# The recurrence's added matrix terms: an addition on VectorE before, a second accumulating product on TensorE after

## The chip, the core and the metric

The kernel runs on one core of a Trainium2 chip. A core has TensorE for matrix products (PE in the profile, its weight loads PEld), VectorE (DVE), ScalarE (ACT), GpSimd (POOL) and SyncE (SP), which issues most of the transfers. Products land in PSUM, eight banks of 128 partitions by 512 float32 values; all else is held in SBUF. The metric is the device time of one execution in microseconds (us). Lower is better.

## The reference

The kernel computes a trunk of two layers on 512 tokens of width 1024 in float32: an RWKV-7 time mixer, a SwiGLU feed-forward layer, a gated spatial mixer (SGU) and a second feed-forward layer, each between two RMS norms. The change is in the time mixer. Each of its 16 heads keeps a state S of 64 by 64 and walks the tokens:

```
S_t = S_{t-1} diag(w_t) + (S_{t-1} a_t) b_t^T + v_t k_t^T
y_t = S_t r_t
```

## The kernel before, in words

**Chunked form.** The recurrence isn't walked token by token. The tokens are cut into 8 chunks of 64. For each head and chunk the kernel builds matrices once, by products, masks and a triangular inverse; then it walks the 8 chunks in order, and in each multiplies those matrices by the state and by the chunk's values. Two heads share the 128 partitions (`hd` is 0 or 1), and two such pairs (`q`) form a block `b`; there are four blocks. `hh` names the first or second four chunks, and `cc` the chunk among the four.

**Stages.** A block runs through P (projections), E (`early`: decay and scaled vectors), F (`front`), B (`back`), S (`scan`) and N (`finish`: group norm, gate). `PLAN` lists the stages of all blocks in the order in which they are written: the ones that matter here are F0 B0 F1 V0 V1 V2 V3 B1 S0 F2 S1 F3 N0 B2 N1 B3 S2 N2 S3 N3, where V are the value projections.

**front** (from line 677) loads for each of the four units (hh, q) of a block a tile MV of 128 by 2x4x2x64 and a tile BX of 128 by 4x4x64, multiplies (lm, line 709), masks the result into MV on VectorE (712), copies parts into LA and BX on ScalarE (715, 716, 726, 727), and lets GpSimd mask one quarter of BX (717). Quarters 2 and 3 of BX get an identity by transfer (703) on the rows of their own head and products on the other rows.

**back** (from line 731) inverts: LA is transposed (LX, line 735), a loop of 15 steps on VectorE (744, 746) solves all diagonal blocks of 16 at once, two transposes follow (749, 750), and a chain of small products with copies between (Qp, Np, Tp, Q2p, T2p) assembles the inverse into bdT. The copies that matter below are the two halves of Q2 (792 on ScalarE, 793 on VectorE) and the two of T2p into bdT (802, one on each engine). Then, for each unit: product mp (807), ScalarE's copy into MVt (809), and for each of the two heads four products gh (814) into one PSUM bank; VectorE adds to the gh bank's first half the quarter 2 or 3 of BX and writes MV[0] (816), and to its second half the old MV[1] and writes MV[1] (817).

**scan** (from line 819) walks the chunks. Each chunk has four products us (843; not in the last chunk), one for each pair and head, whose result times the decay is the next state, in part by VectorE (845) and in part by ScalarE (848), and four products Yp (856). After two chunks ScalarE copies Yp out (858). The values of each chunk are loaded into the state tile by SP (828).

**Who waits for whom.** A scheduler sets each engine's order from the program and a timing model of its own; on the chip each engine then keeps that order. Tiles share buffers: MV, BX and others, such as the tiles of the output projection's operand (oT), share 17 slots, and a tile gets a slot when the last use of an earlier tile is over. A block needs eight slots for MV and BX. The gh banks are two, used in turn.

Of the kernel before, what the change touches and what calls it, by code (L numbers as in the profile page):

```python
# [11 lines left out]
ALU = mybir.AluOpType  # L12

P = 128
# [5 lines left out]
C = 64  # L20
# [62 lines left out]
class Trunk:  # L83
# [287 lines left out]
    def rwkv(self, x0, nxt):  # L371
        nc, i, tc = self.nc, self.i, self.tc
        v, a, g = nc.vector, nc.scalar, nc.gpsimd
        mm = nc.tensor.matmul
        with ExitStack() as ctx:
# [20 lines left out]
            def xslot(name, shape, dt=F32):  # L396
                return self.xp.tile(shape, dt, name=name, tag="x", bufs=TT)

            def gslot(name, shape):
                return self.gp.tile(shape, F32, name=name, tag="gain", bufs=2)  # L400
# [93 lines left out]
            head = [slice(0, 64), slice(64, 128)]  # L494
# [3 lines left out]
            for t, m, w in ((w1m[0], omix, v), (w1m[1], self.vec["mix"], g)):  # L498
                mv = m[:, 3 * KT:5 * KT].rearrange("p (j k) -> p k j", j=2).unsqueeze(3)
# [6 lines left out]
            for j, src in enumerate((hk, hs)):  # L506
                for kt in range(KT):
                    mm(acc, w1m[j][:, kt].rearrange("p j n -> p (j n)"), src(kt), start=j == 0 and kt == 0,
                       stop=j == 1 and kt == KT - 1)
# [220 lines left out]
            def back(b, o):  # L730

                MV, BX, LA, Dm = (o[n] for n in ("MV", "BX", "LA", "Dm"))
# [19 lines left out]
                for hh in range(2):  # L752
                    mt = gslot("MVt", [P, 2, 4, P])
                    for q in q2:
                        pt = self.bank("pl", "mvt")
# [8 lines left out]
                for u in range(16):  # L764
                    for z, hd, x in quarters:
                        mm(Qp[z:z + 32, u * 32:(u + 1) * 32], LAu[z:z + 32, u, 32 * x:32 * x + 32], Dn[z:z + 32, u, x, :],
                           start=True, stop=True)
# [19 lines left out]
                for u in range(16):  # L787
                    for z in (0, 64):
                        mm(Q2p[z + 32:z + 64, u * 32:(u + 1) * 32], LAu[z:z + 32, u, 32:64], Dn2[z:z + 32, u, :],
                           start=True, stop=True)  # L790
# [4 lines left out]
                for u in range(16):  # L795
                    for hd in q2:
                        z = 64 * hd
                        mm(T2p[z:z + 32, u * 32:(u + 1) * 32], Q2[z + 32:z + 64, u, :], bdT[z + 32:z + 64, u, hd, 32:64],
                           start=True, stop=True)
# [4 lines left out]
                for hh, q in units:  # L804
                    mp, mt, mv, bx = self.bank("mp" if b else "pt", "mp"), MVt[hh, q], MV[hh, q], BX[hh, q]
                    for cc in range(4):
                        mm(mp[:, cc * P:(cc + 1) * P], bdT[:, q * NC + 4 * hh + cc].rearrange("p h t -> p (h t)"), mt[:, cc, :],  # L807
                           start=True, stop=True)
                    a.copy(mt.rearrange("p c f -> p (c f)"), mp)
                    for hd in range(2):  # L810
                        rows, other = head[hd], head[1 - hd]
                        gh = self.bank("pt", "gh")
                        for cc in range(4):
                            mm(gh[:, cc * P:(cc + 1) * P], mt[rows, cc, :], bx[rows, 0:2, cc, :], start=True, stop=True)  # L814
                        gv = gh.rearrange("p (c a t) -> p a c t", c=4, a=2)
                        v.tensor_tensor(mv[:, 0, :, hd], gv[:, 0], bx[:, 2 + hd], op=ALU.add)
                        v.tensor_tensor(mv[:, 1, :, hd], gv[:, 1], mv[:, 1, :, hd], op=ALU.add)

            def scan(b, o, then=None):

                MV, pc = o["MV"], o["pc"]
                Y = xslot("Y", [P, TT, 2, P])

                def new_su(c):
                    su = rp.tile([P, 2, 2, C], F32, name="su", tag="su", bufs=4)
                    vv = Vd[c * C:(c + 1) * C, 2 * b * P:2 * b * P + 2 * P].rearrange("t (q h v) -> t q h v", q=2, h=2)
                    for hd in range(2):
                        nc.sync.dma_start(out=su[64 * (1 - hd):64 * (1 - hd) + 64, :, hd, :], in_=vv[:, :, hd, :])
                        if c == 0:
                            g.memset(su[64 * hd:64 * hd + 64, :, hd, :], 0.0)  # L830
                    return su

                su = new_su(0)
                for c in range(NC):
                    hh, cc = c // 4, c % 4
                    tt, par = c // 2, c % 2
                    if c < NC - 1:
                        nsu = new_su(c + 1)
                        us = self.bank("us", "us")
                        for q in q2:  # L840
                            for hd in range(2):
                                rows = slice(64 * hd, 64 * hd + 64)
                                mm(us[rows, q * C:(q + 1) * C], MV[hh, q][:, 0, cc, hd, :], su[:, q, hd, :], start=True, stop=True)

                        v.tensor_tensor(nsu[0:64, :, 0, :], us[0:64, 0:2 * C].rearrange("p (q v) -> p q v", q=2),
                                        pc[0:64, :, c:c + 1].broadcast_to([64, 2, C]), op=ALU.mult)
                        for q in q2:
                            a.activation(nsu[64:128, q, 1, :], us[64:128, q * C:(q + 1) * C], AF.Copy,
                                         scale=pc[64:128, q, c:c + 1])
                    if par == 0:  # L850
                        yp = self.bank("yp", "Yp")
                    yr = slice(64 * par, 64 * par + 64)
                    for q in q2:
                        for hd in range(2):
                            yc = slice(q * P + hd * C, q * P + hd * C + C)
                            mm(yp[yr, yc], MV[hh, q][:, 1, cc, hd, :], su[:, q, hd, :], start=True, stop=True)  # L856
                    if par == 1:
                        a.copy(Y[:, tt].rearrange("p q f -> p (q f)"), yp[:, 0:2 * P])
                    if c < NC - 1:
                        su = nsu  # L860
                    if then and c == NC // 2 - 1:
                        then(Y)
                return Y
# [86 lines left out]
            for n in PLAN:  # L950
                f, b = n[0], int(n[1])
                if f == "P":
                    if xr is None:
                        xr = mixed_split(0, "ssssssss")
                        xx.clear()
                    kr[b] = kr_proj(b)
                elif f == "E":
                    ops[b] = early(b, *kr[b])
                elif f == "X":
                    xs = mixed_split(2, XV)  # L960
                elif f == "V":
                    v_proj(xs, [b])
                elif f == "F":
                    front(b, ops[b])
                elif f == "B":
                    back(b, ops[b])
                elif f == "S":
                    Y[b] = scan(b, ops[b], (lambda y: finish_half(b, ops[b], y, (0, 1))) if b == 3 else None)
                elif b == 3:
                    finish_half(b, ops[b], Y[b], (2, 3))  # L970
                else:
                    finish(b, ops[b], Y[b])
# [166 lines left out]
```

## Time and profile before

| | us |
|---|---|
| median of three runs (1421.11 to 1426.13) | 1424.42 |
| the profiled execution, its own time | 1426.41 |
| its span, first to last instruction | 1424.70 |
| from the first product of block 0's `front` to the end of the last scan, about | 195 to 477 |
| VectorE's additions of lines 816 and 817, 32 each, busy | 13.4 and 13.3 |
| the scan's products of lines 843 and 856, busy | 17.0 and 28.2 |

The page of the profile gives for each engine the busy time and its share, for each line the number of instructions and the mean length of one, and for each wait what ended it. A float32 product of this kernel shows as two records on PE and two on PEld: line 843 has 112 products (7 chunks, 4 products, 4 blocks) and 224 records. "PEclk" is the granted clock of TensorE as a share of full speed. A busy time on PE covers the pipeline's fill and drain, so short gaps are not seen in it.

### The profile page before, as it was taken

How to read it: one execution, taken by the hardware profiler on the slowest of the kernel's cores; microseconds unless marked ns; L12 is line 12 of the kernel's file. 1: busy time of each engine (PE TensorE's matmuls, PEld its weight loads, DVE VectorE, ACT ScalarE, POOL GpSimd, SP SyncE). 2: the span in 40 equal slices, each digit the busy share in tenths (PEclk: the TensorE clock that was granted, in tenths of full speed). 3: DMA queues.
4: the chain of work that ended last, by engine and by line, in shares of the span. 5: the costliest groups of instructions: out<-in, count | busy, mean ns of one | idle time of the engine just before them, and what ended most of it. 6: DMA issues, size and time to landing. Idle time of an engine off the chain costs nothing.

```text
span 1424.7 us, 21481 instructions
## 1 busy us (share of the span) xinstructions
PE 1338.3 (94%) x8472; PEld 1091.2 (77%) x8472; DVE 791.8 (56%) x1318; ACT 569.1 (40%) x1060; POOL 274.5 (19%) x248
## 2 busy tenths in 40 slices
PE   5899997987889979999999999999999999999998
PEld 3576686976768768888888888778888888888886
DVE  6962776388685775554544222865575455443223
ACT  5654665363723363323322122743363232322221
POOL 6154463133311231111111000210121111110000
PEclk9999998987969989999999999999999999999999
DMA  5133467351322423333332232343213333332331
GB/s 157 30 107 92 127 182 200 94 150 43 87 65 88 130 90 104 89 89 103 90 99 94 89 118 74 104 129 109 89 52 112 103 89 89 103 90 103 89 96 67
DMA packets 210324, 143.04 MB, mean 100 GB/s; under 512 B 59664, under 2 KB 185136, under 8 KB 210224
## 3 DMA queue, kind: packets, MB, share of 16 engines
q1 hardware_dynamic: 208544, 135.90, 32.2%
q0 software_dynamic: 1680, 5.77, 1.3%
q8 instruction: 67, 1.10, 0.3%
q14 instruction: 33, 0.27, 0.1%
HBM read 125.39 MB, written 14.16 MB: 98 GB/s over the span
## 4 chain that ended last, share of the span: by engine, by line
PE 77%; DVE 7%; ACT 2%; issue 2%; DMA 2%; POOL 1%; SPq 1%; DVEq 0%; POOLq 0%; ACTq 0%
PE gu L158 12%; PE gu L156 12%; PE gu L157 12%; PE acc L156 8%; PE acc L157 8%; PE acc L158 8%; PE gh L814 2%; PE lm L709 2%; PE u L156 1%; PE u L158 1%; PE u L157 1%; PE Yp L856 1%; PE mp L807 1%; PE proj L158 1%; PE proj L156 1%
## 5 line engine op out<-in xcount | busy, mean ns | idle before, releaser
L131 ACT CAST whi<-wraw 128x1024 fp32r<-128x1024 f32 x161 | 168.8, 1050 | 472.5 <-PE gu L157 257.2
L132 DVE TENSOR_TENSOR wlo<-wraw,whi 128x1024 fp32r<-128x1024 f32 x161 | 246.6, 1532 | 197.2 <-ACT whi L131 193.2
L157 PE MATMUL gu<-hT,whi 128*128 128x512 f32 (+1 forms) x768 | 289.6, 378 | 4.4 <-DVE hT L59 4.4
L156 PE MATMUL gu<-hT,whi 128*128 128x512 f32 (+1 forms) x768 | 290.2, 380 | 0.8 <-ACT hT L57 0.8
L158 PE MATMUL gu<-hT,wlo 128*128 128x512 f32 (+1 forms) x768 | 289.7, 378 | 0.0
L157 PEld LDWEIGHTS gu<-hT,whi 128*128 128x128 f32 x768 | 146.0, 190 | 34.0 <-DVE hT L59 4.7
L156 PEld LDWEIGHTS gu<-hT,whi 128*128 128x128 f32 x768 | 145.8, 191 | 29.5 <-ACT hT L57 1.0
L158 PEld LDWEIGHTS gu<-hT,wlo 128*128 128x128 f32 x768 | 145.8, 190 | 29.0 <-issue 0.2
L157 PE MATMUL acc<-wlo,act 128*128 128x512 f32 x416 | 163.9, 394 | 0.0
L156 PE MATMUL acc<-whi,act 128*128 128x512 f32 x416 | 163.6, 394 | 0.0
L158 PE MATMUL acc<-whi,act 128*128 128x512 f32 x416 | 160.5, 394 | 0.0
L333 POOL TENSOR_TENSOR sg<-sg,hn 128x512 f32<-128x512 f32 x44 | 56.7, 1288 | 422.5 <-DVE sg L332 422.5
L332 DVE TENSOR_TENSOR sg<-sg,gu 128x512 f32<-128x512 f32 x44 | 30.2, 687 | 142.5 <-PE gu L158 141.1
L148 POOL TENSOR_TENSOR wlo<-wraw,whi 128x1024 fp32r<-128x1024 f32 x28 | 70.1, 2505 | 169.9 <-ACT whi L147 151.1
L158 PEld LDWEIGHTS acc<-whi,act 128*128 128x128 f32 x416 | 78.2, 188 | 18.1
L156 PEld LDWEIGHTS acc<-whi,act 128*128 128x128 f32 x416 | 78.2, 188 | 18.0
L157 PEld LDWEIGHTS acc<-wlo,act 128*128 128x128 f32 x416 | 78.1, 188 | 18.0
L330 DVE TENSOR_TENSOR sg<-gu,hn 128x512 f32<-128x512 f32 x44 | 30.4, 691 | 67.8 <-PE gu L158 67.6
L131 ACT CAST act<-sg 128x512 fp32r<-128x512 f32 x52 | 32.3, 622 | 72.2 <-POOL sg L333 58.1
L158 PE MATMUL proj<-xsp,wlo 128*128 128x512 f32 x128 | 53.7, 421 | 0.0
L156 PE MATMUL proj<-xsp,whi 128*128 128x512 f32 x128 | 51.9, 405 | 0.4 <-ACT k L529 0.4
L709 PE MATMUL lm<-MV,ST 128*128 128x128 f32 x256 | 41.6, 316 | 11.2 <-DMA ST<-sb 7.9
(305 smaller groups left out, 2248.8 us busy)
## 6 DMA issues: line engine op xcount, KB each, us to landing
wraw<-in_ffn_w_gate_dram SPq DMA_DIRECT2D x44, 512.0 KB, 3.6
wraw<-in_ffn_w_up_dram SPq DMA_DIRECT2D x44, 512.0 KB
wraw<-in_ffn_w_down_dram SPq DMA_DIRECT2D x44, 512.0 KB, 3.6
wraw<-in_rwkv_w_rkv_dram SPq DMA_DIRECT2D x24, 512.0 KB, 3.5
wraw<-in_sgu_w_in_dram SPq DMA_DIRECT2D x16, 512.0 KB, 3.6
x<-in_x_dram SPq DMA_DIRECT2D x8, 512.0 KB, 3.7
MV<-sa SPq DMA_DIRECT2D x64, 64.0 KB, 2.6
ST<-sb SPq DMA_DIRECT2D x8, 512.0 KB, 4.5
```

Of the source, the lines that this page charges most:

```text
L131: self.nc.scalar.copy(hi, src)
L132: self.nc.vector.tensor_tensor(lo, src, hi.bitcast(F32), op=ALU.subtract)
L148: nc.gpsimd.tensor_tensor(lo, raw, hi.bitcast(F32), op=ALU.subtract)
L156: mm(out, lhs[0], rhs[0], start=start, stop=False)
L157: mm(out, lhs[0], rhs[1], start=False, stop=False)
L158: mm(out, lhs[1], rhs[0], start=False, stop=stop)
L330: nc.vector.tensor_tensor(sg, pp[0], yb, op=ALU.mult)
L332: nc.vector.tensor_tensor(sg, sg, pp[1], op=ALU.mult)
L333: nc.gpsimd.tensor_tensor(sg, sg, yb, op=ALU.mult)
L709: mm(lm[:, cc * P:(cc + 1) * P], st[:, cc].rearrange("p n t -> p (n t)"), mv[:, :, cc, hd, :], start=True, stop=True)
L807: mm(mp[:, cc * P:(cc + 1) * P], bdT[:, q * NC + 4 * hh + cc].rearrange("p h t -> p (h t)"), mt[:, cc, :], start=True, stop=True)
L814: mm(gh[:, cc * P:(cc + 1) * P], mt[rows, cc, :], bx[rows, 0:2, cc, :], start=True, stop=True)
```

## The change

Nothing else than `back` and `scan` is touched. In `back` the additions of lines 816 and 817 are gone. The gh products of both heads are written first, each into its own bank, and then ScalarE makes four plain copies: the first half of each bank into MV[0], the second half into quarter `hd` of BX, whose old contents the products have read by then. MV[1] keeps what `front` put there. In `scan` each product becomes two that accumulate in PSUM: the state times quarter 2 or 3 of BX and then times MV[0], and the state times MV[1] and then times quarter `hd` of BX. BX is thus still read at the last chunk; before, its last reader was in `back`.

```diff
                     a.copy(mt.rearrange("p c f -> p (c f)"), mp)
+                    ghs = [self.bank("pt", "gh") for _ in range(2)]
                     for hd in range(2):
-                        rows, other = head[hd], head[1 - hd]
-                        gh = self.bank("pt", "gh")
                         for cc in range(4):
-                            mm(gh[:, cc * P:(cc + 1) * P], mt[rows, cc, :], bx[rows, 0:2, cc, :], start=True, stop=True)
-                        gv = gh.rearrange("p (c a t) -> p a c t", c=4, a=2)
-                        v.tensor_tensor(mv[:, 0, :, hd], gv[:, 0], bx[:, 2 + hd], op=ALU.add)
-                        v.tensor_tensor(mv[:, 1, :, hd], gv[:, 1], mv[:, 1, :, hd], op=ALU.add)
+                            mm(ghs[hd][:, cc * P:(cc + 1) * P], mt[head[hd], cc, :], bx[head[hd], 0:2, cc, :], start=True, stop=True)
+                    for hd in range(2):
+                        gv = ghs[hd].rearrange("p (c a t) -> p a c t", c=4, a=2)
+                        a.copy(mv[:, 0, :, hd], gv[:, 0])
+                        a.copy(bx[:, hd], gv[:, 1])
...
-                                mm(us[rows, q * C:(q + 1) * C], MV[hh, q][:, 0, cc, hd, :], su[:, q, hd, :], start=True, stop=True)
+                                out = us[rows, q * C:(q + 1) * C]
+                                mm(out, BX[hh, q][:, 2 + hd, cc, :], su[:, q, hd, :], start=True, stop=False)
+                                mm(out, MV[hh, q][:, 0, cc, hd, :], su[:, q, hd, :], start=False, stop=True)
...
-                            mm(yp[yr, yc], MV[hh, q][:, 1, cc, hd, :], su[:, q, hd, :], start=True, stop=True)
+                            mm(yp[yr, yc], MV[hh, q][:, 1, cc, hd, :], su[:, q, hd, :], start=True, stop=False)
+                            mm(yp[yr, yc], BX[hh, q][:, hd, cc, :], su[:, q, hd, :], start=False, stop=True)
```

The scheduler also orders the engines' work anew. Three places show it.

VectorE in block 1's inverse, from ScalarE's and VectorE's copies of Q2 (line 793) to the last copy into bdT (line 802), which the products mp wait for. Names: tm and Dm belong to the solving loop of the next block, mu, va, nr and Y to block 0's group norm. Before, 18 instructions stand between the two copies; the last nine and the copy are

```order
L712 TENSOR_TENSOR MV<-lm,mk_126 64x4x2x64
L173 SCALAR_TENSOR_TENSOR nr_t<-nr_t,nr_a 128x16
L746 TENSOR_TENSOR Dm<-Dm,tm 128x2x13x3
L174 SCALAR_TENSOR_TENSOR nr_y<-nr_t,nr_y 128x16
L744 TENSOR_TENSOR tm<-LX,Dm 128x2x48
L885 TENSOR_TENSOR Y<-Y,nr_y 128x1024
L746 TENSOR_TENSOR Dm<-Dm,tm 128x2x12x4
L744 TENSOR_TENSOR tm<-LX,Dm 128x2x55
L746 TENSOR_TENSOR Dm<-Dm,tm 128x2x11x5
L802 COPY bdT<-T2p 32x16x32
```

and in the changed kernel all of it is

```order
L793 COPY Q_2948<-Q2p 32x512
L881 TENSOR_REDUCE mu<-Y 128x16
L882 TENSOR_SCALAR mu<-mu 128x16
L883 TENSOR_TENSOR Y<-Y,mu 128x1024
L712 TENSOR_TENSOR MV<-lm,mk_126 64x4x2x64
L887 TENSOR_REDUCE va<-hn 128x16
L802 COPY bdT<-T2p 32x16x32
```

The solving loop of the next block now begins after the copy into bdT, and block 0's group norm begins where it had been half done.

TensorE in the first scan, the state's step from the fourth chunk to the fifth. Before, with `front`'s products lm of block 2 behind it:

```order
L843 MATMUL us_3123<-su_3104,MV_1478 64x64 x2
L843 MATMUL us_3123<-su_3104,MV_1485 64x64 x2
L856 MATMUL Yp_3115<-su_3104,MV_1485 64x64
L709 MATMUL lm_3230<-MV_3191,ST_3189 128x128 x4
L709 MATMUL lm_3239<-MV_3191,ST_3189 128x128 x4
```

and in the changed kernel, where the eight rows of the same step are followed by eight Yp rows and then by two rows of lm:

```order
L845 MATMUL us_3147<-su_3120,BX_1514 64x64
L846 MATMUL us_3147<-su_3120,MV_1478 64x64
L845 MATMUL us_3147<-su_3120,BX_1514 64x64
L846 MATMUL us_3147<-su_3120,MV_1478 64x64
L845 MATMUL us_3147<-su_3120,BX_1545 64x64
L846 MATMUL us_3147<-su_3120,MV_1485 64x64
L845 MATMUL us_3147<-su_3120,BX_1545 64x64
L846 MATMUL us_3147<-su_3120,MV_1485 64x64
```

Each product of the step is two rows now; the order of the stages around them is nearly the same.

SP in the second scan, where it loads block 3's MV (line 690) and BX and the state tiles su. Before:

```order
L690 DMA MV_3483<-sa_120 64x4x64 x4
L603 DMA g2_4748<-in_rwkv_g2_dram 128x256
L690 DMA MV_3492<-sa_120 64x4x64 x2
L828 DMA su_3405<-Vd_116 64x2x64 x2
L690 DMA MV_3492<-sa_120 64x4x64 x2
L936 DMA od_125<-ob_3703 128x512
L909 DMA g2r_4754<-in_rwkv_g2_dram 32x256 x3
L828 DMA su_3421<-Vd_116 64x2x64 x2
L690 DMA MV_3499<-sa_120 64x4x64 x2
```

and in the changed kernel, where su_3561 is the second scan's last state tile:

```order
L690 DMA MV_3603<-sa_120 64x4x64
L829 DMA su_3561<-Vd_116 64x2x64 x2
L690 DMA MV_3603<-sa_120 64x4x64 x3
L690 DMA MV_3612<-sa_120 64x4x64 x4
L690 DMA MV_3619<-sa_120 64x4x64 x4
L703 DMA BX_3632<-ident_79 64x4x64 x2
L703 DMA BX_3663<-ident_79 64x4x64 x2
L703 DMA BX_3694<-ident_79 64x4x64 x2
L703 DMA BX_3725<-ident_79 64x4x64 x2
L891 DMA hn_4258<-Vd_116 128x4x256
L829 DMA su_4711<-Vd_116 64x2x64 x2
```

Three of block 3's four MV tiles, spread through the second scan before, now stand behind its last state tile, because BX of blocks 1 and 2 holds its slots longer.

More of the change, by code (lines that the diff above doesn't have):

```diff
@@ L809, in back @@
                     a.copy(mt.rearrange("p c f -> p (c f)"), mp)
+                    ghs = [self.bank("pt", "gh") for _ in range(2)]
                     for hd in range(2):
-                        rows, other = head[hd], head[1 - hd]
-                        gh = self.bank("pt", "gh")
                         for cc in range(4):
-                            mm(gh[:, cc * P:(cc + 1) * P], mt[rows, cc, :], bx[rows, 0:2, cc, :], start=True, stop=True)
-                        gv = gh.rearrange("p (c a t) -> p a c t", c=4, a=2)
-                        v.tensor_tensor(mv[:, 0, :, hd], gv[:, 0], bx[:, 2 + hd], op=ALU.add)
-                        v.tensor_tensor(mv[:, 1, :, hd], gv[:, 1], mv[:, 1, :, hd], op=ALU.add)
+                            mm(ghs[hd][:, cc * P:(cc + 1) * P], mt[head[hd], cc, :], bx[head[hd], 0:2, cc, :], start=True, stop=True)
[3 more added lines that the diff above has]
+                        a.copy(bx[:, hd], gv[:, 1])
             def scan(b, o, then=None):
-                MV, pc = o["MV"], o["pc"]
+                MV, BX, pc = o["MV"], o["BX"], o["pc"]
                 Y = xslot("Y", [P, TT, 2, P])
```

## The prediction

> **What bounds the kernel now.** I read the page's busy line and its chain first, to learn which engine sets the end of the whole program, and then cut the time mixer's scans into stages, because a share over the whole span hides them. The page's busy line, and the chain of waits that ended last:
>
> ```profile
> PE 1338.3 (94%) x8472; PEld 1091.2 (77%) x8472; DVE 791.8 (56%) x1318; ACT 569.1 (40%) x1060; POOL 274.5 (19%) x248
> ...
> PE 77%; DVE 7%; ACT 2%; issue 2%; DMA 2%; POOL 1%; SPq 1%; DVEq 0%; POOLq 0%; ACTq 0%
> ```
>
> TensorE is busy 94% of the span and holds 77% of the chain. So work added to TensorE is likely to cost its full length, and work taken from VectorE pays only in the 7%. The view of six stretches (busy time of each engine, number of records, granted clock) says where either holds:
>
> ```profile
> core 0: us, PE busy (x) PEld busy (x) DVE busy (x) ACT busy (x) POOL busy (x), PEclk, DMA share, GB/s
> 260.00:311.00 51.00, 49.45 (x619) 44.86 (x618) 31.51 (x69) 30.75 (x81) 13.35 (x22) 0.98 0.48 131
> 311.00:345.00 34.00, 21.82 (x411) 19.53 (x401) 26.83 (x55) 13.02 (x32) 12.71 (x13) 0.63 0.21 59
> 345.00:380.00 35.00, 33.98 (x592) 28.68 (x591) 19.45 (x45) 19.88 (x59) 5.45 (x11) 0.97 0.28 67
> 380.00:412.00 32.00, 20.97 (x224) 17.72 (x214) 31.50 (x65) 12.66 (x22) 13.45 (x8) 0.63 0.28 92
> 412.00:441.00 29.00, 27.18 (x536) 22.12 (x536) 13.01 (x26) 11.35 (x26) 0.00 (x0) 0.88 0.19 57
> 441.00:511.00 70.00, 68.46 (x538) 55.59 (x536) 52.46 (x128) 29.41 (x73) 19.77 (x18) 1.00 0.36 111
> ```
>
> There are two regimes. In stretches 1, 3, 5 and 6 TensorE idles 1.55, 1.02, 1.82 and 1.54 us: it is the bound, and VectorE has room. In 2 and 4, where the inverses of blocks 1 and 2 are assembled, TensorE idles 12.2 and 11.0 us at a clock of 0.63, and VectorE is busy 26.83 of 34 and 31.50 of 32 us: there a short VectorE queue is worth something. The scans, and so the new products, lie mostly in the first regime.
>
> **The change, part by part.** The sum goes against the profiled execution's own 1426.41 us, which is 1.99 above the median of the three runs.
>
> *The 240 added products.* 7 x 4 x 4 = 112 for the state and 8 x 4 x 4 = 128 for the output, each as large as those of these groups:
>
> ```profile
> L856 PE MATMUL Yp<-su,MV 128*64 128x64 f32 x256 | 28.2, 232 | 0.0
> L843 PE MATMUL us<-su,MV 128*64 128x64 f32 x224 | 17.0, 235 | 0.0
> ```
>
> The mean of 232 to 235 ns is a record's length with fill and drain, and overlaps its neighbours; the spacing is what an added one costs. A chunk of the last scan, and one of the first, on TensorE's timeline:
>
> ```profile
> 461.39 0.45 PE L843 MATMUL us<-su,MV 128*64 128x64 f32 x8
> 461.67 0.63 PE L856 MATMUL Yp<-su,MV 128*64 128x64 f32 x8
> 462.23 0.50 PE L156 MATMUL acc<-whi,oT 128*128 128x512 f32 x1
> ...
> 296.31 0.22 PE L843 MATMUL us<-su,MV 128*64 128x64 f32 x1
> ...
> 298.79 0.50 PE L856 MATMUL Yp<-su,MV 128*64 128x64 f32 x5
> ...
> 299.19 0.40 PE L843 MATMUL us<-su,MV 128*64 128x64 f32 x7
> ```
>
> From 461.39 to the next work at 462.23, 16 records (8 products) take 0.84 us, 0.105 a product. Inside the seven records that end 0.40 after 299.19, the last is 0.22 long, so the others begin 0.18/6 = 0.03 apart, 0.06 a product while another group's records lie between. I take 0.09, nearer to the whole chunk: 240 x 0.09 = **+21.6** (14.4 to 25.2). Nearly all of it lands on a full TensorE. One part does not: the first scan's last chunks run around the gap before this group,
>
> ```profile
> 315.14 0.34 PE L766 MATMUL Qp<-hn,LA 32*32 32x32 f32 x9 [4.05 <-issue]
> ```
>
> whose products now stand ahead of those chunks: some 12 added products fit in the idle 4.05 us, 12 x 0.09 = **-1.1** (0 to -2).
>
> *The 64 additions leave VectorE, 64 copies come to ScalarE.*
>
> ```profile
> L816 DVE TENSOR_TENSOR MV<-gh,BX 128x256 f32<-128x256 f32 x32 | 13.4, 419 | 9.0 <-PE gh L814 8.8
> L817 DVE TENSOR_TENSOR MV<-gh,MV 128x256 f32<-128x256 f32 x32 | 13.3, 415 | 0.0
> ...
> L858 ACT COPY Y<-Yp 128x256 f32<-128x256 f32 x16 | 6.0, 373 | 8.0 <-PE Yp L856 7.7
> ```
>
> VectorE loses 26.7 us of work. In the first regime this is worth nothing. A ScalarE copy of the same shape from PSUM takes 373 ns, so ScalarE gets 64 x 0.373 = 23.9 us. Its busy times of 13 to 31 us in stretches of 29 to 70 cover them: 0. Without that cover, the next unit's copy of mp waits behind four copies, 1.5 us, and TensorE with it; were that to happen at every third of the 16 units, it would be +8 (I allow +5, since the gh banks of the next unit can be filled meanwhile only if ScalarE has emptied them).
>
> *VectorE's order in the two inverses.* mp waits for VectorE's half of the copy into bdT. In block 1 and block 2:
>
> ```profile
> 312.38 1.20 DVE L877 TENSOR_REDUCE mu<-Y 128x16 f32<-128x1024 f32 x1
> ...
> 316.35 1.23 DVE L879 TENSOR_TENSOR Y<-Y,mu 128x1024 f32<-128x1024 f32 x1
> ...
> 319.06 1.22 DVE L883 TENSOR_REDUCE va<-hn 128x16 f32<-128x1024 f32 x1
> ...
> 328.23 0.70 DVE L793 COPY Q<-Q2p 32x512 f32<-32x512 f32 x1
> ...
> 336.68 0.69 DVE L802 COPY bdT<-T2p 32x512 f32<-32x512 f32 x1
> ...
> 385.17 0.70 DVE L793 COPY Q<-Q2p 32x512 f32<-32x512 f32 x1
> ...
> 396.22 0.69 DVE L802 COPY bdT<-T2p 32x512 f32<-32x512 f32 x1
> ```
>
> ```profile
> 337.42 2.07 PE L807 MATMUL mp<-MVt,bdT 128*128 128x128 f32 x8 [5.25 <-DVE bdT L802]
> ...
> 396.96 2.07 PE L807 MATMUL mp<-MVt,bdT 128*128 128x128 f32 x8 [7.30 <-DVE bdT L802]
> ```
>
> In block 1, 7.75 us lie between the end of the Q copy (328.93) and the start of the bdT copy. The changed order leaves five instructions there: the three group-norm passes of 1.20, 1.23 and 1.22, one mask of 0.68 (row below, line 712) and a small one, 4.5 us. That is **-3** (0 to -6, where T2p's own end is met; a mask that waits for lm makes it 0). In block 2, 10.35 us of solving steps and norm go, and nine instructions stand there now, among them two masks, the next block's LX (1.95 below) and two passes of Y, about 7.3 us: **-3** (0 to -7). The group norm that is pushed behind is late next; its result feeds the output projection, which is filler.
>
> *The gh banks.* Emptied by VectorE, they make TensorE wait now and then, and the products run at two speeds:
>
> ```profile
> 293.75 1.71 PE L814 MATMUL gh<-BX,MVt 64*128 64x128 f32 x16
> ...
> 341.15 3.10 PE L814 MATMUL gh<-BX,MVt 64*128 64x128 f32 x16
> ...
> 357.76 1.79 PE L814 MATMUL gh<-BX,MVt 64*128 64x128 f32 x16 [0.70 <-DVE MV L817]
> ```
>
> 0.70 us in block 1 and the like goes: **-1** (0 to -1.5). In block 2, where VectorE is full, the second bank is empty only after the addition at
>
> ```profile
> 406.33 0.41 DVE L817 TENSOR_TENSOR MV<-gh,MV 128x256 f32<-128x256 f32 x1
> ```
>
> though its products had started at 399.77 (below) and ended 3.09 later: **-2** (0 to -4).
>
> ```profile
> 399.77 3.09 PE L814 MATMUL gh<-BX,MVt 64*128 64x128 f32 x16 [0.73 <-ACT MVt L809]
> ```
>
> *The clock.* The same 16 records take 1.71 us at 293.75 and 3.10 at 341.15, after the 5.25 us gap. With shorter gaps some of it comes back: **-1.5** (0 to -4; all of it is a rival).
>
> *The slots.* BX is now held until the scan. Block b+2's eight slots come free with chunks 4 and 8 of block b's scan, and SP issues the loads of block 3's last units behind the state tiles. One issue of BX's identities, and where the chain of block 3's `front` ends now:
>
> ```profile
> 366.06 3.90 SPq L703 DMA_DIRECT2D BX<-ident  x6
> ...
> 378.43 0.68 DVE L712 TENSOR_TENSOR MV<-lm,mk 64x512 f32<-64x512 f32 x1 [1.78 <-PE lm L709]
> ...
> 380.16 1.95 DVE L735 STREAM_TRANSPOSE LX<-LA 128x1024 f32<-128x1024 f32 x1
> ```
>
> One such issue (3.9 us) behind the state tiles, with TensorE's filler of the output projection late as well because its operand waits for a slot: **+4** (0 to +12). Queued behind a late load on SP are the next state tiles, and the scan waits for these.
>
> *Sum.* 21.6 - 1.1 - 3 - 3 - 1 - 2 - 1.5 + 4 = +14.0. On 1426.4 this is 1440.4, and less 1.99 the median is **1438**, 1.0% slower. All low ends together give 14.4 - 2 - 6 - 7 - 1.5 - 4 - 4 = -10 (1414); all high ends 25.2 + 12 + 5 = +42 (1467).
>
> **The rivals.**
>
> *A: faster, by the clock.* If the gaps before mp get so short that the clock stays up, the busy 21.82 and 20.97 us of stretches 2 and 4 shrink by their missing share of 0.37, 8.1 + 7.8 = 15.9 us in place of my 1.5, and the sum is -0.4; with the gaps themselves at their low ends (-13 in place of -6) it is -7.4, a median near **1417**. For it: 3.10 against 1.71. Against it: the solving loop and the masks still come before mp in block 2, and 4.05 us before Qp is of its own. It decides once no gap in these stretches exceeds some 2 us. The Trainium skill, page "TensorE: Matmul & The Clock Gate", section "HAM oscillation — how this bites in real kernels", says that idle gaps over about 3.4 us throttle the engine to half rate again; the 5.25 and 7.30 us gaps, with 3.10 and 3.09 us products behind them, agree, and by that rule this rival needs both gaps under 3.4.
>
> *B: no change.* Busy TensorE is not full TensorE. Weight loads are busy only 44.86 of 51, 28.68 of 35, 22.12 of 29 and 55.59 of 70 us, so some 34 us have no load, and if half of the added products (10.8 us) slip in there, the sum is +3.2 and the median near **1428**. Against it: the chunk above takes 0.84 us for 8 products with nothing between. The Trainium skill, page "Perfetto Trace Analysis", section "Identifying the Most-Contended Engine", calls the matmul row's busy share a poor sign of utilisation and the weight loads' share the better one; its measure here would be 77%, not 94%.
>
> *C: much slower, by the slots.* Block 3's last three units can be loaded only once the second scan has ended: an issue of 3.9 us, and then three `front` units in a row on TensorE, about 3 us each by the 3.10 us that 16 records take at the low clock, before the solve that now starts at 380.16: +13 where I have +4, and no gain in block 2 (-3 and -2 gone): +29, a median near **1453**. For it: VectorE's bdT copy of block 2 stands behind block 3's LX in the order. Against it: MV was held until the scan already.
>
> *D: the second product of a pair waits for the first's result* in PSUM: 0.235 - 0.09 = 0.145 more for each of 240, +35, near **1473**. Against it, the projections add into the same cells every 394 ns record without a gap:
>
> ```profile
> L157 PE MATMUL acc<-wlo,act 128*128 128x512 f32 x416 | 163.9, 394 | 0.0
> ```
>
> **How the numbers follow.** Chances: the forecast 0.53, A 0.20, B 0.13, C 0.11, D 0.03. The forecast's own range, 1429 to 1448, comes from its larger terms missing one way each. For 8 in 10 I go down to A's value and up past C's: **1416 to 1456**. A difference under 0.3% (4.3 us, 1420.1 to 1428.7) can't be told from none. Faster takes A and a little of the forecast's lower end, 0.21; same takes B and the rest of that end, 0.16; slower 0.63.
>
> **What would show it.** Right: the state's and output's lines with twice the records and a mean still near 0.23 us; stretches like 1, 3 and 5 longer by 5 us each with TensorE as full as before; gaps before mp of 2 to 5 us and a clock still under 0.8 there; ScalarE's new copies near 373 ns and never what mp waits for. Wrong: a clock near 1 in the inverses (A); stretches no longer than before with twice the products (B); block 3's LX more than 8 us behind its old place beside the scan (C); pairs spaced over 0.15 us (D). The size fails above all if a chunk's eight added records cost more than they do in a row, because each half of a pair loads other weights.

## The result, and the profile after

The changed kernel takes 1433.16 us (median of six runs, 1429.08 to 1435.03), the kernel before in the same series 1424.03. The ratio is 1.0057, with a 95% interval of 1.0033 to 1.0081: slower by 8.1 us (4.7 to 11.5), and clear of no change. The forecast was 1438, slower, with 13.6 us in place of the 8 to 9 measured. The profiled execution took 1430.03 us, the second lowest of the six.

The page's busy line and the chain of waits of the changed kernel:

```profile
PE 1351.9 (95%) x8952; PEld 1106.6 (77%) x8952; DVE 772.5 (54%) x1254; ACT 588.3 (41%) x1124; POOL 272.9 (19%) x248
...
PE 71%; DVE 5%; issue 1%; ACT 1%; DMA 0%; POOL 0%; DVEq 0%; POOLq 0%; ACTq 0%
```

The 480 records are there, and so are the 64 additions that VectorE no longer makes and the 64 copies of ScalarE. But TensorE's busy time rose by only 13.6 us. The six stretches of the prediction, in the same columns:

```profile
260.00:311.00 51.00, 50.91 (x691) 46.70 (x684) 26.01 (x52) 31.45 (x87) 12.70 (x21) 0.97 0.42 126
311.00:345.00 34.00, 25.92 (x489) 23.20 (x488) 24.17 (x39) 17.71 (x47) 12.92 (x12) 0.90 0.26 60
345.00:380.00 35.00, 33.89 (x642) 29.03 (x643) 18.34 (x42) 18.27 (x55) 4.93 (x10) 0.90 0.25 62
380.00:412.00 32.00, 26.59 (x273) 22.85 (x272) 28.66 (x60) 20.99 (x49) 12.68 (x9) 0.73 0.39 115
412.00:441.00 29.00, 25.88 (x671) 23.28 (x669) 12.63 (x19) 14.26 (x37) 0.40 (x2) 0.88 0.18 54
441.00:511.00 70.00, 68.88 (x572) 56.57 (x571) 43.04 (x100) 27.86 (x69) 14.95 (x14) 1.00 0.34 108
```

The two stretches around the inverses changed most: the second from 21.82 busy us at a clock of 0.63 to 25.92 at 0.90, the fourth from 20.97 at 0.63 to 26.59 at 0.73. To compare whole time mixers I take the window from the first product lm of block 0 to the first transpose (line 218) behind the output projection. First the kernel before, then the changed one:

```profile
195.52:507.75 312.23, 273.05 (x3614) 236.05 (x3615) 214.29 (x440) 148.92 (x360) 86.11 (x99) 0.88 0.38 108
```

```profile
194.73:513.61 318.88, 289.00 (x4094) 253.42 (x4095) 195.00 (x376) 168.10 (x424) 83.32 (x99) 0.91 0.37 106
```

The window is 6.65 us longer: 15.95 more busy, 9.3 less idle (39.2 to 29.9). Busy time times clock tells how much work there is at full speed: 273.05 x 0.88 = 240 before, 289.00 x 0.91 = 263 after. So about 23 us of work came in (21 when it is added up over windows of half a microsecond, 244 and 265), near the 21.6 of the sum, and part of it was paid by a higher clock and by idle time. These are single executions. Two kernels of the experiments whose medians lie 2 us apart (VectorE's order alone, in its two forms) have windows of 307.5 and 317.7 us, as their profiled executions took 1421.49 and 1431.45. So I lean on the windows for kinds, and on the timed series for sizes.

The groups that answer to those of the prediction; first the changed kernel's:

```profile
L859 PE MATMUL Yp<-su,MV 128*64 128x64 f32 x256 | 35.9, 235 | 0.3 <-DVE su L848 0.3
L860 PE MATMUL Yp<-su,BX 128*64 128x64 f32 x256 | 34.4, 230 | 1.1 <-ACT BX L818 1.1
L814 PE MATMUL gh<-BX,MVt 64*128 64x128 f32 x256 | 28.6, 294 | 0.2 <-ACT MVt L809 0.2
L845 PE MATMUL us<-su,BX 128*64 128x64 f32 x224 | 20.8, 240 | 2.4 <-DMA su<-Vd 2.3
L807 PE MATMUL mp<-MVt,bdT 128*128 128x128 f32 x128 | 19.4, 298 | 0.5 <-DVE bdT L802 0.5
L846 PE MATMUL us<-su,MV 128*64 128x64 f32 x224 | 19.2, 228 | 0.0
L818 ACT COPY BX<-gh 128x256 f32<-128x256 f32 x32 | 12.3, 383 | 2.0 <-PE gh L814 1.8
L817 ACT COPY MV<-gh 128x256 f32<-128x256 f32 x32 | 12.0, 376 | 6.4 <-PE gh L814 6.3
```

and of the kernel before the two whose work did not change:

```profile
L814 PE MATMUL gh<-BX,MVt 64*128 64x128 f32 x256 | 33.4, 313 | 1.8 <-ACT MVt L809 1.1 <-DVE MV L817 0.7
L807 PE MATMUL mp<-MVt,bdT 128*128 128x128 f32 x128 | 22.8, 333 | 12.8 <-DVE bdT L802 12.8
```

The waits ahead of mp went from 12.8 to 0.5 us, further down than forecast (2 to 5 us left in each inverse), and the same gh and mp products take 8.2 us less, by the clock. ScalarE's copies last 376 and 383 ns, as forecast. A new wait stands at line 845, for the state's values. TensorE's timeline there, SP's issues, and the clock in short windows around it:

```profile
385.00 0.44 PE L845 MATMUL us<-su,BX 128*64 128x64 f32 x2 [2.29 <-DMA su<-Vd]
385.59 3.78 PE L709 MATMUL lm<-MV,ST 128*128 128x128 f32 x16
```

```profile
373.04 7.66 SPq L703 DMA_DIRECT2D BX<-ident  x8
...
381.48 6.86 SPq L829 DMA_DIRECT2D su<-Vd  x8
```

```profile
378.00:382.00 4.00, 3.38 (x83) 2.98 (x83) 3.84 (x6) 3.24 (x8) 0.00 (x0) 1.00 0.33 67
382.00:385.00 3.00, 0.71 (x18) 0.46 (x16) 2.73 (x10) 2.05 (x6) 0.32 (x1) 0.79 0.71 210
385.00:389.00 4.00, 4.00 (x20) 3.88 (x20) 3.90 (x4) 1.71 (x5) 4.00 (x4) 0.50 0.18 37
```

Eight issues of BX's identities stand in one run on SP ahead of the state tiles, TensorE waits 2.29 us for a state tile, and its clock, 1.00 until 382, is 0.50 from 385 on. The low clock of the fourth stretch thus begins at another wait now. Block 3's LX is late, as the prediction's term on the slots had it: it starts 14.9 us later against the window's start than before.

```profile
394.30 1.99 DVE L735 STREAM_TRANSPOSE LX<-LA 128x1024 f32<-128x1024 f32 x1 [0.70 <-ACT LA L715]
```

### The profile page after: what moved, and what is told of

Its sections match the earlier page's. It is cut to its first block, busy times and chain, and to the rows that moved or that the text cites. A ratio compares the mean times of both kernels' runs of the same rounds, so it can differ in the third digit from the quotient of the medians.

```text
span 1428.3 us, 22384 instructions
## 1 busy us (share of the span) xinstructions
PE 1351.9 (95%) x8952; PEld 1106.6 (77%) x8952; DVE 772.5 (54%) x1254; ACT 588.3 (41%) x1124; POOL 272.9 (19%) x248
## 3 DMA queue, kind: packets, MB, share of 16 engines
q8 instruction: 71, 1.16, 0.3%
## 4 chain that ended last, share of the span: by engine, by line
PE 71%; DVE 5%; issue 1%; ACT 1%; DMA 0%; POOL 0%; DVEq 0%; POOLq 0%; ACTq 0%
PE gu L157 12%; PE gu L158 12%; PE gu L156 11%; PE acc L156 9%; PE acc L157 9%; PE acc L158 8%; PE gh L814 1%; PE u L158 1%; PE u L157 1%; PE u L156 1%; PE Yp L859 1%; DVE x L273 1%; PE mp L807 1%; PE Yp L860 1%; PE us L845 1%
```

## The experiments

Each stood beside the kernel before on the same chip. Ratios are given with their 95% interval; microseconds are the ratio's distance from one times 1425.

**The products alone.** The kernel before, with a product against a tile of zeros behind each product of the scan. Nothing else of the change is made.

```diff
+            Zt = rp.tile([P, 8], F32, name="Z", tag="Z", bufs=1)
+            g.memset(Zt, 0.0)
+            Z = Zt[:, 0:1].broadcast_to([P, C])
...
-                            mm(yp[yr, yc], MV[hh, q][:, 1, cc, hd, :], su[:, q, hd, :], start=True, stop=True)
+                            mm(yp[yr, yc], MV[hh, q][:, 1, cc, hd, :], su[:, q, hd, :], start=True, stop=False)
+                            mm(yp[yr, yc], Z, su[:, q, hd, :], start=False, stop=True)
```

(and the same at the state's product)

> The kernel before, with the 240 products of the change added in the scan, but their stationary operand is a tile of zeros: no copies, no additions removed, no buffer held. Theory (a product costs 0.09 us on a full TensorE, and the shorter waits ahead of mp give back 9 to 10 us): +12 to +22 us, 1.009 to 1.015, since VectorE's order in block 1 is also shorter here (5 instructions ahead of the copy into bdT). Rival (a product costs only 0.04 us and nothing was given back): +8 to +10 us, 1.006.

Measured: 1.0060 (1.0039 to 1.0080), +8.6 us, the number of the rival. Its window, and the zero products' groups:

```profile
192.58:517.22 324.64, 290.43 (x4095) 255.49 (x4096) 217.34 (x440) 149.62 (x360) 82.47 (x99) 0.90 0.37 104
```

```profile
L862 PE MATMUL Yp<-su,Z 128*64 128x64 f32 x256 | 34.8, 232 | 0.0
L848 PE MATMUL us<-su,Z 128*64 128x64 f32 x224 | 19.5, 231 | 0.0
```

They last as long as the real ones (228 to 240 ns). Busy time times clock is 290.43 x 0.90 = 261, 21 more than before, and idle time is 34.2 in place of 39.2. So the products, without one addition removed, cost what the whole change costs. But they did not come alone: the scheduler ordered VectorE's work anew here too, and the waits ahead of mp are 3.6 us in place of 12.8:

```profile
L807 PE MATMUL mp<-MVt,bdT 128*128 128x128 f32 x128 | 20.9, 313 | 3.6 <-DVE bdT L802 3.6
```

**`back` alone.** Both gh banks first and ScalarE's four copies, as in the changed kernel, with the scan of before. The added terms are left out of the result.

```diff
-                        v.tensor_tensor(mv[:, 0, :, hd], gv[:, 0], bx[:, 2 + hd], op=ALU.add)
-                        v.tensor_tensor(mv[:, 1, :, hd], gv[:, 1], mv[:, 1, :, hd], op=ALU.add)
+                        a.copy(mv[:, 0, :, hd], gv[:, 0])
+                        a.copy(bx[:, hd], gv[:, 1])
```

> The change's `back` (both gh banks first, ScalarE's four copies, no additions) with the scan of before: the added terms are left out of the state and of the output, and 240 products with them. Theory: -8 to -12 us (0.992 to 0.994), the waits and the clock alone, with a gap of under 2 us before mp in block 1. Rival (nothing was given back): 0, 1.000. If ScalarE's copies cost: above 1.000.

Measured: 0.9988 (0.9967 to 1.0009), -1.7 us: no difference that can be told, and not the -8 to -12 of the theory. The waits ahead of mp did get shorter:

```profile
333.06 1.16 PE L807 MATMUL mp<-MVt,bdT 128*128 128x128 f32 x8 [2.65 <-DVE bdT L802]
...
392.00 2.08 PE L807 MATMUL mp<-MVt,bdT 128*128 128x128 f32 x8 [4.77 <-DVE bdT L802]
```

```profile
193.65:507.92 314.27, 272.95 (x3614) 236.26 (x3615) 194.40 (x376) 168.90 (x424) 84.25 (x99) 0.88 0.38 108
```

5.25 became 2.65 and 7.30 became 4.77, nearly the 3 us each of the sum, yet the window's idle time is 41.3 us against 39.2: it stands elsewhere now. VectorE is 20 us less busy, and nothing came of it.

**The wait ahead of mp, taken off VectorE.** The kernel before with both halves of the copy into bdT on ScalarE:

```diff
-                for hd, cp in ((0, a.copy), (1, v.tensor_copy)):
+                for hd, cp in ((0, a.copy), (1, a.copy)):
```

> The kernel before, with VectorE's half of the copy into bdT given to ScalarE; nothing else. Theory (the wait ahead of mp in blocks 1 and 2 is VectorE's queue, and the low clock follows from it): gaps before mp of 5.25 and 7.30 fall under 2, TensorE's clock in the two stretches rises from 0.63 to over 0.8, -9 to -14 us (0.990 to 0.994). Rival (the next wait, on VectorE's masks or gh additions, takes its place): 0 to -4 us.

Measured: 0.9986 (0.9969 to 1.0003), -2.0 us, as the rival said. TensorE and ScalarE in block 1:

```profile
329.14 1.16 PE L807 MATMUL mp<-MVt,bdT 128*128 128x128 f32 x8
340.95 3.09 PE L814 MATMUL gh<-BX,MVt 64*128 64x128 f32 x16 [10.65 <-ACT MVt L809]
```

```profile
336.87 0.63 ACT L715 COPY LA<-lm 32x256 f32<-32x256 f32 x2 [7.79 <-DVE MV L712]
339.66 0.63 ACT L715 COPY LA<-lm 32x256 f32<-32x256 f32 x2 [2.15 <-DVE MV L712]
340.31 0.59 ACT L809 COPY MVt<-mp 128x512 f32<-128x512 f32 x1
```

mp now runs 8 us earlier with no wait, and the next link takes the whole of it: ScalarE's copy of mp stands behind copies of block 2's `front` which wait for VectorE's masks, and gh waits 10.65 us.

The same edit in the changed kernel:

> The changed kernel with VectorE's half of the copy into bdT given to ScalarE. Theory: in the changed kernel these gaps are closed already (0.54 us in block 1), so it differs from it by under 3 us: 1.004 to 1.006 of the kernel before. Rival (block 2's copy, 8.8 us behind the Q copy there, still costs): 1.000 to 1.003.

1.0054 (1.0037 to 1.0070), the same as the changed kernel's 1.0057, as expected.

**The same 240 products in one scan.** Four zero products behind each of the 60 products of one block's scan, none in the other three: in the last block,

```diff
+                            if b == 3:
+                                mm(yp[yr, yc], MV[hh, q][:, 1, cc, hd, :], su[:, q, hd, :], start=True, stop=False)
+                                mm(yp[yr, yc], Z, su[:, q, hd, :], start=False, stop=False)
...
+                                mm(yp[yr, yc], Z, su[:, q, hd, :], start=False, stop=True)
```

> The kernel before, with 240 zero products again, but all of them in the last block's scan: four behind each of its 28 state and 32 output products. That scan lies in a stretch where TensorE idles 1.5 of 70 us, and VectorE's order in the earlier blocks is that of before. Theory now (a product costs some 0.09 us where TensorE is full; spread over the four scans much of it only fills what was idle): +17 to +24 us, 1.012 to 1.017. Rival (a product costs only 0.04 us anywhere): +7 to +10 us, 1.006.

in the second block,

> The same 240 zero products, all in the scan of the second block, beside the inverse of the third, where TensorE idles 11 us and its clock is low. Theory now (idle time is filled): +3 to +12 us, 1.002 to 1.008, and less than in the last scan. Rival (0.04 us anywhere): +7 to +10 us and as much as in the last scan. If each costs its length here too: +17 to +24 us.

and in the first:

> 240 zero products, all in the first block's scan, beside the inverse of block 1, four behind each product. If products fill TensorE's 12 idle us in that stretch: +8 to +14 us, 1.006 to 1.010. If they delay what waits for the scan, as in the second scan: +20 to +29 us, 1.014 to 1.020.

Measured: last 1.0162 (1.0140 to 1.0184), +23.1 us; second 1.0198 (1.0173 to 1.0223), +28.2; first 1.0292 (1.0262 to 1.0322), +41.6. Their windows, in the same order:

```profile
194.10:528.80 334.70, 296.51 (x4095) 259.24 (x4096) 213.59 (x440) 149.53 (x360) 86.46 (x99) 0.90 0.36 101
```

```profile
194.33:535.43 341.10, 289.75 (x4095) 254.83 (x4096) 215.75 (x440) 149.37 (x360) 81.24 (x98) 0.90 0.36 99
```

```profile
192.77:552.77 360.00, 303.97 (x4094) 265.15 (x4095) 218.04 (x441) 149.91 (x360) 84.10 (x100) 0.87 0.34 94
```

In the last scan, where the waits ahead of mp are the 12.8 us of before, a product costs 23.1 / 240 = 0.096 us, and idle time stays (38.2): that is the price of the sum. My expectation for the second scan, that idle time beside an inverse would be filled, was wrong: idle rose to 51.4 us there and to 56.0 with the first scan, and both times lie above every range that I had given. Block 2's mp, which started 201.4 us into the window before, starts at 229.9 and 243.7. The longest wait of TensorE in these two windows, second scan and then first, stands shortly ahead of that mp, at the transposes of the group norm's result (yt; 0.61 us at most before):

```profile
416.87 1.11 PE L945 MATMUL yt<-ident,Y 128*128 128x128 f32 x4 [10.57 <-DVE Y L919]
```

```profile
426.58 1.12 PE L945 MATMUL yt<-ident,Y 128*128 128x128 f32 x4 [8.49 <-DVE Y L919]
```

So products that lengthen one scan push back what is queued behind it; that this is the whole of the difference isn't shown. The same 240 products thus cost 8.6, 23, 28 or 42 us by where they stand, each time with the order that the scheduler made around them.

**480 products over the four scans**, two behind each:

> 480 zero products spread over the four scans, two behind each product. Theory now (the first 240 take up idle time, the second find less): +20 to +32 us over before, 1.014 to 1.022, more than twice the first 240. Rival (0.04 us anywhere): +17 to +20 us, 1.012 to 1.014.

1.0193 (1.0168 to 1.0217), +27.5 us: three times the first 240, so the second 240 cost 18.9.

```profile
193.42:532.62 339.20, 311.19 (x4575) 275.51 (x4576) 212.92 (x440) 150.49 (x360) 84.12 (x99) 0.92 0.36 100
```

Idle time goes 39.2, 34.2, 28.0 with none, 240 and 480 spread products, the clock 0.88, 0.90, 0.92, and the waits ahead of mp 12.8, 3.6, 0. The price is no constant 0.04: by the timed series the first 240 are cheap and the second are not. The windows, single executions, show it less (12.4 us longer with the first, 14.6 more with the second).

**BX held until the scan**, with additions as before, and 16 small products into unread columns:

```diff
+                    if cc == 3:
+                        for q in q2:
+                            mm(yp[yr, 2 * P + q * C:2 * P + q * C + C], BX[hh, q][:, 3, cc, :], su[:, q, 1, :], start=True, stop=True)
```

> The kernel before, with BX held until the scan by 16 small products, one for each unit behind the last chunk that uses it, into unread columns of the output's bank; additions and everything else as before. Prediction's term: +4 us (0 to +12), 1.003, with block 3's LX some 10 us later than before. Rival (the later loads cost nothing, since MV was held until then already): 0 to +2 us, 1.000 to 1.001.

1.0006 (0.9991 to 1.0021), +0.9 us, the rival's number. LX of block 3 did start 12 us later in the window (196.7 against 184.6), but the end did not follow. Here too VectorE's order moved with it: the waits ahead of mp are 1.6 us.

**VectorE's order alone.** Block 2's solve may begin only behind block 1's copy into bdT, so that block 1 gets the short queue of the changed kernel:

```diff
                 LX = e2("LX", (P, 2, 528))
+                if b in (2,):
+                    v.tensor_copy(full(LX)[64:96, 0], bdT[64:96, 0, 1, 32:64])
```

> The kernel before, in which block 2's solve on VectorE can begin only behind the last copy of block 1's inverse into bdT (a copy of 32 by 32 values into LX, overwritten at once, makes the order); no products, no other change. It gives block 1 the short VectorE queue that the changed kernel has. Theory O (what the changed kernel gets back is this order): mp of block 1 starts 7 to 9 us earlier, and the time falls by 6 to 10 us, 0.993 to 0.996. Rival F (closing this wait only moves the idle time, since the solve that was hidden in it is then due later; what the change gets back is idle time that the products fill): 0 to -2 us, 0.9985 to 1.000.

and with `(2, 3)` in place of `(2,)`:

> The same, and block 3's solve too begins only behind block 2's copy into bdT, as it nearly does in the changed kernel. Theory O: 8 to 14 us less, 0.990 to 0.994. Rival F: within 2 us of the kernel before, with LX of block 3 10 us later and the gap ahead of block 2's mp under 3 us.

0.9990 (0.9971 to 1.0008) and 1.0003 (0.9986 to 1.0021): -1.4 and +0.4 us. In the first the wait ahead of block 1's mp is gone and that of block 2 is what it was:

```profile
392.10 2.08 PE L809 MATMUL mp<-MVt,bdT 128*128 128x128 f32 x8 [7.43 <-DVE bdT L804]
```

In the second 3.97 us of that wait remain, where I expected under 3. Neither gives the 6 to 14 us of theory O. For the first, rival F's -2 to 0 holds the estimate, though the interval reaches to -4.1.

**Half of the change.** Only the state's products in pairs; VectorE keeps the addition into MV[1]:

```diff
-                        v.tensor_tensor(mv[:, 0, :, hd], gv[:, 0], bx[:, 2 + hd], op=ALU.add)
+                        a.copy(mv[:, 0, :, hd], gv[:, 0])
...
+                                mm(out, BX[hh, q][:, 2 + hd, cc, :], su[:, q, hd, :], start=True, stop=False)
+                                mm(out, MV[hh, q][:, 0, cc, hd, :], su[:, q, hd, :], start=False, stop=True)
```

> Half of the change: only the state's products come in pairs (112 added), ScalarE copies MV[0], and VectorE keeps the addition into MV[1]. The changed kernel's rows show the two heads' state products side by side, 0.058 us each, and the output's 0.117: by them these 112 cost 6.5 us on a full TensorE and the other 128 cost 15. With the change's net of 9 us shared in that proportion: +1 to +5 us, 1.001 to 1.0035. Rival (0.09 each and nothing given back): +10 us, 1.007.

1.0026 (1.0007 to 1.0045), +3.7 us, as expected for a third of the added TensorE time. The spacing behind that expectation, in a chunk of the changed kernel's last scan:

```profile
461.39 0.34 PE L845 MATMUL us<-su,BX 128*64 128x64 f32 x4
...
461.86 0.28 PE L859 MATMUL Yp<-su,MV 128*64 128x64 f32 x2
461.98 0.28 PE L860 MATMUL Yp<-su,BX 128*64 128x64 f32 x2
462.09 0.28 PE L859 MATMUL Yp<-su,MV 128*64 128x64 f32 x2
```

The eight state products take 461.86 - 461.39 = 0.47 us, 0.059 each; each output product takes 0.12.

## Why the prediction came out as it did

Direction, range and the forecast case held; the time was 5 us too high. But run one by one, two terms of the sum came out wrong in opposite ways, and a third with them, so that the total's nearness is in part luck:

| part of the change | in the sum | by itself on the chip |
|---|---|---|
| products, with the first gap (-1.1) and the clock (-1.5) | +19.0 | +8.6 (5.6 to 11.4) |
| `back`: order in the inverses and gh banks | -9 | -1.7 (-4.7 to 1.3) |
| slots | +4 | +0.9 (-1.3 to 3.0) |
| together | +14.0 | +7.8 |
| the change | | +8.1 (4.7 to 11.5) |

The parts add up to the whole within their intervals, which leave room for some microseconds either way. But they are not clean parts, because the scheduler moved VectorE's order in most of these kernels. The waits are those ahead of mp, the idle time is TensorE's in the window, and all are us:

| kernel | added products | waits | idle | time |
|---|---|---|---|---|
| before | 0 | 12.8 | 39.2 | |
| `back` alone | 0 | 7.4 | 41.3 | -1.7 |
| copy into bdT on ScalarE | 0 | 2.0 | 41.3 | -2.0 |
| VectorE's order alone, block 2 | 0 | 7.7 | 37.9 | -1.4 |
| the same, blocks 2 and 3 | 0 | 4.0 | 42.5 | +0.4 |
| BX held | 16 | 1.6 | 39.8 | +0.9 |
| last scan | 240 | 12.8 | 38.2 | +23.1 |
| second scan | 240 | 6.1 | 51.4 | +28.2 |
| first scan | 240 | 2.8 | 56.0 | +41.6 |
| half of the change | 112 | 0.5 | 36.2 | +3.7 |
| spread | 240 | 3.6 | 34.2 | +8.6 |
| the change | 240 | 0.5 | 29.9 | +8.1 |
| the change, copy on ScalarE | 240 | 0.4 | 32.4 | +7.7 |
| spread, two behind each | 480 | 0.0 | 27.9 | +27.5 |

Shorter waits without products, or with 16 small ones, save 2 us at most by the estimates. The one kernel with products and without shorter waits, that of the last scan, pays their full price. Idle time falls by more than 2 us only where spread products and shorter waits come together.

*"240 x 0.09 = +21.6", and "nearly all of it lands on a full TensorE".* The price was right: 0.096 in the last scan, and rows spaced 0.059 for the state and 0.12 for the output, on average 0.09. The second half was the step that failed. Spread over four scans, and with the order that came with them, a good half of the price does not reach the end. The windows show two ways: less idle time (39.2 to 34.2), and a higher mean clock (0.88 to 0.90). At the clock of before the 290.43 busy us of the zero kernel would have been 290.43 x 0.90 / 0.88 = 297, about 7 more (3 to 10, since the clock has two digits; windows of half a microsecond, weighted by busy time, give 0.907 and 0.894, and 4 us), where the sum had 1.5 for the clock. The forecast looked for idle time only in the two large gaps and the one ahead of Qp, and let the products fill no other.

A rival to this reading was not tried: spread products cost their price too, and a closed wait pays once there are products to run in its place. By the sum's own terms the zero kernel is then at 21.6 - 1.1 - 1.5 and less its 9.2 of closed waits, +9.8, inside its interval. Half of the change speaks against it: its 112 products cost 6.6 to 10.1 us (0.059 or 0.09 each), less than the 12.3 of its closed waits, and it is slower all the same. A kernel with spread products and VectorE's order of before would decide.

*"-3", "-3", "-1" and "-2" for VectorE's order and the gh banks.* Each wait was read rightly and did close (12.8 to 0.5 ahead of mp), but a closed wait was taken for time saved. `back` alone, the short queue alone and the copy on ScalarE show that, with no products added, other instructions wait instead, most plainly gh with its 10.65 us. The line ahead of a stall told what ended it, not what it was worth.

*"ScalarE's copies: 0"* holds: 376 and 383 ns, and `back` alone is not slower.

*"+4" for the slots* was too high by some 3 us, or by 1 if the shorter waits of that kernel saved as much as elsewhere (2.0): the late LX of block 3 came as described, and 2.29 us of waiting for a state tile behind the loads with it, but the end did not follow. Its row of 3.90 us is six issues, not one. Its bound of +12 and rival C's price are out; by its own terms that price is +28, near 1452, and not +29.

*The rivals.* A asked for the clock to stay up in both inverses. It rose to 0.90 and 0.73, so part of A's mechanism was at work, but not enough to turn the sign. Closed waits alone leave the window's clock at 0.88 and 0.89 (copy on ScalarE, VectorE's order alone); it is 0.90 to 0.92 only with products added. B, that the products slip in cheaply, had half of the truth: they do when spread (8.6 us), though room between weight loads is not enough for it: the last scan's stretch has such room (55.59 of 70 us busy), and there they cost their full length. D is out: pairs are spaced like single products.

What stays open: why the spread products raise the clock by that much, and how much of their low price they owe to VectorE's new order. That order alone gives at most 4 us, but the two weren't separated within one kernel. That a chunk of a scan has room for 0.7 us more (8 products at 0.09) but not for four times as much would explain the four prices of the same products; it is argued from them, not measured.

No version tried beats the kernel before by more than its uncertainty; the best, the copy on ScalarE, is at 0.9986 with an interval up to 1.0003.

## What to carry to other kernels

Price added TensorE work where it will stand: the same 240 products cost 8.6 us spread thin, with the order that came with them, and 42 us in one early scan. Before counting a stall as a gain, ask which instruction waits next once it is gone; an experiment that removes only that stall tells it for the price of one line. A sum that comes out right in total can still be two errors that cancel, and only parts run by themselves show that. Whether a part ran by itself is read from its trace: here the scheduler closed waits in kernels that were meant only to add products.

## What was unexpected of the hardware

**The length of a wait does not tell by itself whether the clock falls.** In the changed kernel the mean clock from 382 to 385 us is 0.79, and 0.50 after it: it fell from 1.00 near 383.7, some 1.0 us into the wait of 2.29, with 0.62 us idle shortly before. In `back` alone the clock is 1.00 from 330 to 337 us, through the wait of 2.65 ahead of mp, and mp takes 1.16 us; behind the wait of 4.77 it takes 2.08. And in the kernel before, the clock was down ahead of the 5.25 us wait, which begins at 332.18, and not by it as the prediction had it:

```profile
330.00:334.00 4.00, 2.18 (x18) 1.84 (x11) 3.90 (x17) 1.19 (x3) 0.34 (x2) 0.52 0.00 0
```

The Trainium skill, page "TensorE: Matmul & The Clock Gate", section "HAM oscillation — how this bites in real kernels", puts the limit at idle gaps over about 3.4 us; no gap of that length stands just ahead of either fall, and the clock fell all the same. In the changed kernel a stretch that was mostly idle (0.71 of 3 us busy) went with it. What exactly decides isn't isolated here.

**Two heads' products run side by side.** State products for the two halves of the output partitions take 0.059 us each, and output products that all write the same half 0.12. The Trainium skill, page "TensorEngine Tiling (Array Packing)", section "When to Use Tiling", lists 2x column tiling for a stationary side of 64 columns; the rows agree with a factor of two, and in this chunk have it where neighbours write different partitions.

**A small VectorE instruction can take as long as the GpSimd instruction beside it.** The changed kernel's VectorE, and then its GpSimd:

```profile
387.49 2.27 DVE L172 TENSOR_TENSOR nr_t<-nr_y 128x16 f32<-128x16 f32 x1
389.80 0.17 DVE L173 SCALAR_TENSOR_TENSOR nr_t<-nr_t,nr_a 128x16 f32<-128x16 f32 x1
```

```profile
387.38 2.35 POOL L903 TENSOR_TENSOR hn<-hn,gn 128x1024 f32<-128x1024 f32 x1
```

The product of 16 elements a partition takes 2.27 us and ends with GpSimd's instruction; its neighbour takes 0.17. In the kernel before, a step of the solve in the queue ahead of block 1's bdT is of the same kind, where its neighbour takes 0.28:

```profile
334.00 2.35 DVE L744 TENSOR_TENSOR tm<-LX,Dm 128x110 f32<-128x110 f32 x1
336.37 0.28 DVE L746 TENSOR_TENSOR Dm<-Dm,tm 128x110 f32<-128x110 f32 x1
```

```profile
333.87 2.34 POOL L900 TENSOR_TENSOR Y<-Y,gn 128x1024 f32<-128x1024 f32 x1 [3.65 <-DVE Y L885]
```

Some 2 of the 7.75 us that the prediction counted there were this, and not the instructions. That GpSimd causes it is read from the times that coincide; it wasn't tried.
